# Interleaving two tensors: output rows stored in four pieces of 8 KiB, two tiles taking turns within a row

## The chip, the core and the metric

The kernel runs on one core of a Trainium2 chip. The core has engines that compute (of these only VectorE, called DVE in the profile, does work here), an on-chip memory of 128 partitions (SBUF), and 16 DMA engines that move data between SBUF and the off-chip memory (HBM, "dram" in the names). A transfer is issued by an engine's instruction queue: here SyncE (SP) issues the loads and ScalarE (ACT) the stores. Each issue is spread over the 16 DMA engines, 8 partitions each, and runs beside whatever else they hold. When it has landed, it raises a semaphore by 16, and other engines wait for that.

The metric is the device time of one execution, in microseconds (us).

## The reference

```python
def reference(x, y):                       # each (32, 256, 1024) float32
    batch, seq, dim = x.shape
    result = np.zeros((batch, seq, dim * 2), dtype=np.float32)
    result[..., 0::2] = x
    result[..., 1::2] = y
    return result
```

Element i of x goes to place 2i of the output and element i of y to place 2i + 1. Nothing is calculated: 33.6 MB of x and 33.6 MB of y are read, and 67.1 MB are written, 134.2 MB in all. Since the last dimension is only doubled, the tensors can be taken as flat: flat element j of x and of y becomes the flat output pair (2j, 2j + 1).

## The kernel before

The flat tensors are cut into n = 8 steps (k = 0 to 7). In a step each of the 128 partitions takes W = 8192 consecutive elements of x (a row of 32 KiB), the same of y, and yields 16384 consecutive elements of the output (64 KiB in HBM). SBUF holds two x tiles, two y tiles (b = k % 2) and two output tiles `ot[0]` and `ot[1]`, each 128 x 8192 float32. A step's output doesn't fit one output tile, so it is made in two halves, h = 0 and h = 1: half h takes columns h * 4096 to (h + 1) * 4096 of x and y, fills `ot[h]`, and is stored to the h-th 32 KiB of each 64 KiB output row.

Everything is written out by hand, one queue per kind of work, with semaphores between them:

- SP issues the loads. The first x tile comes as two halves of its columns (L42 and L43, semaphores `xsem[0]` and `hsem`); all other loads are a whole tile of 4 MiB (x at L50, y at L53). From k = 2 on, the x load waits until the third of the four copies of step k - 2 is done, and the y load until the fourth is, because these free the buffers (`woven` counts copies).
- VectorE makes four copies in each step: for each half, x into the even places of `ot[h]` (L67) and y into the odd places (L70). Ahead of the first it waits for the x tile (for h = 0; in the first step, half 1 waits for `hsem`), and, from the second step on, until the store that used `ot[h]` before has landed (`osem[h]`). The y copy of half 0 also waits for the y tile.
- ACT waits for the two copies of a half and issues its store (L83). The very first store is issued as two column ranges, 8 KiB and 24 KiB of each row (L77 and L81), with a semaphore of its own (`qsem`) for the first.

At the end ACT and SP wait for the last stores, and the semaphores are set back. After the program is built, `tile_interleave_kernel` moves the first two SP loads to the front of the program, ahead of the opening barrier.

Of the kernel before, what the change touches and what calls it, by code (L numbers as in the profile page):

```python
# [3 lines left out]


def _interleave(nc, x, y, out):
    P = 128
    W = 8192
    H = W // 2  # L10

    total = 1
    for s in x.shape:
        total *= s
    n = total // (P * W)
    assert n * P * W == total

    def rows(ap, names, k):
        flat = ap.rearrange("b s d -> (b s d)")
        return flat[k * names : (k + 1) * names].rearrange("(p w) -> p w", p=P)  # L20

    fp32 = mybir.dt.float32
    xt = [nc.alloc_sbuf_tensor(f"xt{b}", [P, W], fp32).ap() for b in (0, 1)]
    yt = [nc.alloc_sbuf_tensor(f"yt{b}", [P, W], fp32).ap() for b in (0, 1)]
    ot = [nc.alloc_sbuf_tensor(f"ot{b}", [P, W], fp32).ap() for b in (0, 1)]

    xsem = [nc.alloc_semaphore(f"xsem{b}") for b in (0, 1)]
    hsem = nc.alloc_semaphore("hsem")
    qsem = nc.alloc_semaphore("qsem")
    ysem = [nc.alloc_semaphore(f"ysem{b}") for b in (0, 1)]  # L30
    woven = nc.alloc_semaphore("woven")
    osem = [nc.alloc_semaphore(f"osem{b}") for b in (0, 1)]


    cuts = [0, W // 4, W]
    parts = [slice(a, b) for a, b in zip(cuts, cuts[1:])]

    xs = [rows(x, P * W, k) for k in range(n)]
    ys = [rows(y, P * W, k) for k in range(n)]
    os_ = [rows(out, 2 * P * W, k) for k in range(n)]  # L40

    nc.sync.dma_start(out=xt[0][:, :H], in_=xs[0][:, :H]).then_inc(xsem[0], 16)  # L42
    nc.sync.dma_start(out=xt[0][:, H:], in_=xs[0][:, H:]).then_inc(hsem, 16)  # L43

    for k in range(n):
        b = k % 2
        if k >= 2:
            nc.sync.wait_ge(woven, 4 * (k - 2) + 3)
        if k:
            nc.sync.dma_start(out=xt[b], in_=xs[k]).then_inc(xsem[b], 16)  # L50
        if k >= 2:
            nc.sync.wait_ge(woven, 4 * (k - 2) + 4)
        nc.sync.dma_start(out=yt[b], in_=ys[k]).then_inc(ysem[b], 16)  # L53

    for k in range(n):
        b = k % 2
        for h in (0, 1):
            c = slice(h * H, (h + 1) * H)
            if h == 0:
                nc.vector.wait_ge(xsem[b], 16 * (k // 2 + 1))  # L60
            elif k == 0:
                nc.vector.wait_ge(hsem, 16)
            if k:
                nc.vector.wait_ge(osem[h], 16 * k)
            if (k, h) == (1, 0):
                nc.vector.wait_ge(qsem, 16)
            nc.vector.tensor_copy(out=ot[h][:, 0::2], in_=xt[b][:, c]).then_inc(woven, 1)  # L67
            if h == 0:
                nc.vector.wait_ge(ysem[b], 16 * (k // 2 + 1))
            nc.vector.tensor_copy(out=ot[h][:, 1::2], in_=yt[b][:, c]).then_inc(woven, 1)  # L70

    for k in range(n):
        for h in (0, 1):
            nc.scalar.wait_ge(woven, 4 * k + 2 * h + 2)
            if (k, h) == (0, 0):
                for c in parts[:-1]:
                    nc.scalar.dma_start(  # L77
                        out=os_[k][:, c], in_=ot[h][:, c]
                    ).then_inc(qsem, 16)
                c = parts[-1]  # L80
                nc.scalar.dma_start(out=os_[k][:, c], in_=ot[h][:, c]).then_inc(osem[h], 16)  # L81
                continue
            nc.scalar.dma_start(  # L83
                out=os_[k][:, h * W : (h + 1) * W], in_=ot[h]
            ).then_inc(osem[h], 16)

    nc.scalar.wait_ge(osem[0], 16 * n)
    used = sorted(s.num for s in [*xsem, hsem, qsem, *ysem, woven, osem[0]])
    assert used == list(range(used[0], used[-1] + 1)), used
    nc.scalar.sem_clear(range(used[0], used[-1] + 1))  # L90
    nc.sync.nop(nofuse=True).wait_op(osem[1], 16 * n, "sem-ge").then_inc(
        osem[1], -16 * n
    )


def kernel(tc, x, y, out):
    nc = tc.nc
    tc.close()
    tc.compile()

    _interleave(nc, x, y, out)

    blocks = nc.main_func.blocks
    for engine in (mybir.EngineType.SP, mybir.EngineType.SP):
        opening = blocks[0].instructions
        at, moved = next(
            (b, i)
            for b in blocks[1:]
            for i in b.instructions
            if i.engine == engine and i.opcode == "DMACopy"  # L110
        )
        assert not (moved.sync_info and moved.sync_info.on_wait)
        body = at.instructions
        body.remove(moved)
        gate = next(
            n
            for n, i in enumerate(opening)
            if i.engine == engine and i.opcode == "Drain"
        )
        opening.insert(gate, moved)  # L120
        at.instructions = body
        blocks[0].instructions = opening


# [1 line left out]
_INS = ['x', 'y']  # L126
_OUTS = [((32, 256, 2048), 'float32')]


# [23 lines left out]
```

## Time and profile before

| | us |
|---|---|
| median of 3 runs (lowest, highest) | 314.22 (314.19, 314.39) |
| span of the profiled execution (first to last instruction) | 312.9 |
| VectorE busy, 32 copies | 72.0 |
| one x copy / one y copy, mean | 2.295 / 2.288 |
| VectorE idle, waiting for stores to land | 206.5 |
| store of 4 MiB, issue to landing, median | 34.1 |
| x load / y load of 4 MiB, issue to landing, median | 24.3 / 41.5 |

The profiled execution's own time is known as its span only; the three runs were timed without a profile, and their median is 1.3 us longer than that span. A view of the profile is a page (shares of engines, DMA traffic in 40 slices, the chain of work that ended last, groups of instructions, DMA issues) or an answer of the trace behind it: groups by line, the timeline, tables by stretches of time. "DMA share" is the mean busy share of the 16 DMA engines. The trace also keeps a record of each DMA packet: its queue, start, duration and size. The profile names the loads' queue q1 and the stores' queue q10. "Issue to landing" counts the time in which a transfer waits behind earlier ones.

### The profile page before, as it was taken

To read this page: it belongs to the slowest core of one execution; us is meant where nothing else is said; L and a number is where in the kernel's file an instruction comes from. 1 tells how busy PE (TensorE), PEld (TensorE's weight loads), DVE (VectorE), ACT (ScalarE), POOL (GpSimd) and SP (SyncE) were. 2 spreads that over 40 slices of the span, in tenths; PEclk is the share of its full clock that TensorE was granted. 3 is DMA by queue.
4 is the path that set the end of the run, shared out by engine and by line. 5 is a ranking of instruction groups with operands and counts; after the bars stand their busy time and mean duration, and the time that the engine had idled before them with its cause. 6 is when DMAs were issued, how large, how long until landed. Compare 5 with 4: busy or idle time off the path is not lost.

```text
span 312.9 us, 114 instructions
## 1 busy us (share of the span) xinstructions
DVE 72.0 (23%) x32; POOL 0.2 (0%) x4
## 2 busy tenths in 40 slices
DVE  0216000501305023050220503205032050415410
POOL 0000000000000000000000000000000000000000
DMA  8999999999999999999999999999999999999998
GB/s 337 467 402 436 436 402 419 452 457 415 427 444 411 461 402 469 402 469 402 469 402 465 406 440 432 423 448 402 469 402 469 402 469 402 469 402 448 423 423 381
DMA packets 4896, 134.22 MB, mean 429 GB/s; under 512 B 544, under 2 KB 544, under 8 KB 544
## 3 DMA queue, kind: packets, MB, share of 16 engines
q1 hardware_dynamic: 2448, 67.11, 50.1%
q10 hardware_dynamic: 2448, 67.11, 49.7%
HBM read 67.11 MB, written 67.11 MB: 429 GB/s over the span
## 4 chain that ended last, share of the span: by engine, by line
DMA 82%; DVE 12%; issue 0%
DMA out_dram<-ot 76%; DMA yt<-in_y_dram 6%; DVE ot L70 6%; DVE ot L67 6%
## 5 line engine op out<-in xcount | busy, mean ns | idle before, releaser
L67 DVE COPY ot<-xt 128x4096 f32<-128x4096 f32 x16 | 36.7, 2295 | 213.8 <-DMA out_dram<-ot 206.5
L70 DVE COPY ot<-yt 128x4096 f32<-128x4096 f32 x16 | 36.6, 2288 | 12.3 <-DMA yt<-in_y_dram 12.3
L137 POOL MEMSET const-bfloat16-1.0<- 128x1 bf16 x1 | 0.1, 103 | 0.0
L137 POOL MEMSET const-uint8-127<- 128x1 uint8 x1 | 0.1, 102 | 0.0
L137 POOL MEMSET const-float32-0.0<- 128x1 f32 x1 | 0.1, 100 | 0.2 <-issue 0.2
L137 POOL MEMSET const-float32-1.0<- 128x1 f32 x1 | 0.1, 99 | 0.0
## 6 DMA issues: line engine op xcount, KB each, us to landing
out_dram<-ot ACTq DMA_DIRECT2D x15, 4096.0 KB, 34.1
yt<-in_y_dram SPq DMA_DIRECT2D x8, 4096.0 KB, 41.5
xt<-in_x_dram SPq DMA_DIRECT2D x7, 4096.0 KB, 24.3
xt<-in_x_dram SPq DMA_DIRECT2D x2, 2048.0 KB, 9.5
out_dram<-ot ACTq DMA_DIRECT2D x1, 3072.0 KB, 32.8
out_dram<-ot ACTq DMA_DIRECT2D x1, 1024.0 KB, 16.3
```

What stands on the lines that cost most here:

```text
L67: nc.vector.tensor_copy(out=ot[h][:, 0::2], in_=xt[b][:, c]).then_inc(woven, 1)
L70: nc.vector.tensor_copy(out=ot[h][:, 1::2], in_=yt[b][:, c]).then_inc(woven, 1)
L137: nc = _bacc.Bacc("TRN2", target_bir_lowering=False, num_devices=1)
```

## The change

The two output tiles of a step no longer hold the first and the second half of each output row. The 64 KiB of a row are seen as S = 4 groups of two pieces of 8 KiB (G = 2048 elements): `ot[0]` holds the first piece of every group and `ot[1]` the second. Accordingly half h copies, from x and from y, four runs of 1024 elements that lie 2048 elements apart. So a store still reads one contiguous row of 32 KiB per partition in SBUF, but writes four pieces of 8 KiB that lie 16 KiB apart in HBM.

The store is issued through a new function, `_split_copy`, which builds the DMA instruction itself, with the SBUF side described as one row of 8192 elements and the HBM side as four pieces of 2048. The first store is still issued in two parts: the first piece of each row by the ordinary call, and then three pieces (one read of 24 KiB, three writes) by `_split_copy`. Since half 0 of the first step now takes elements from the whole x tile, the first copy waits for both halves of the first x load. The number and order of the instructions on every queue stay as they were.

```diff
+def _split_copy(engine, out, in_):
+
+    return engine.add_instruction(
+        mybir.InstDMACopy(
+            mode="Copy",
+            name=engine.bass.get_next_instruction_name(),
+            engine=engine.engine,
+            ins=engine.lower_ap_dma(in_.rearrange("p (o w) -> p o w", o=1)),
+            outs=engine.lower_ap_dma(out),
+            queue=QUEUES[engine.engine],
+        )
+    )
...
+    S = 4
+    G = W // S
...
-    os_ = [rows(out, 2 * P * W, k) for k in range(n)]
+    os_ = [
+        rows(out, 2 * P * W, k).rearrange("p (s h g) -> p s h g", h=2, g=G)
+        for k in range(n)
+    ]
...
-            c = slice(h * H, (h + 1) * H)
+            pairs = ot[h].rearrange("p (s w two) -> p s w two", s=S, two=2)
+            xc, yc = (
+                t[b].rearrange("p (s h w) -> p s h w", s=S, h=2)[:, :, h] for t in (xt, yt)
+            )
             if h == 0:
                 nc.vector.wait_ge(xsem[b], 16 * (k // 2 + 1))
-            elif k == 0:
-                nc.vector.wait_ge(hsem, 16)
+                if k == 0:
+                    nc.vector.wait_ge(hsem, 16)
...
-            nc.vector.tensor_copy(out=ot[h][:, 0::2], in_=xt[b][:, c]).then_inc(woven, 1)
+            nc.vector.tensor_copy(out=pairs[:, :, :, 0], in_=xc).then_inc(woven, 1)
...
-            nc.vector.tensor_copy(out=ot[h][:, 1::2], in_=yt[b][:, c]).then_inc(woven, 1)
+            nc.vector.tensor_copy(out=pairs[:, :, :, 1], in_=yc).then_inc(woven, 1)
...
             if (k, h) == (0, 0):
-                for c in parts[:-1]:
-                    nc.scalar.dma_start(
-                        out=os_[k][:, c], in_=ot[h][:, c]
-                    ).then_inc(qsem, 16)
-                c = parts[-1]
-                nc.scalar.dma_start(out=os_[k][:, c], in_=ot[h][:, c]).then_inc(osem[h], 16)
-                continue
-            nc.scalar.dma_start(
-                out=os_[k][:, h * W : (h + 1) * W], in_=ot[h]
+                nc.scalar.dma_start(out=os_[k][:, 0, h], in_=ot[h][:, :G]).then_inc(
+                    qsem, 16
+                )
+                first = 1
+            _split_copy(
+                nc.scalar, os_[k][:, first:, h], ot[h][:, first * G :]
             ).then_inc(osem[h], 16)
```

## The prediction

> **What bounds the kernel now.** I read the page's head and its DMA part first.
>
> ```profile
> span 312.9 us, 114 instructions
> ...
> DVE 72.0 (23%) x32; POOL 0.2 (0%) x4
> ...
> DMA  8999999999999999999999999999999999999998
> GB/s 337 467 402 436 436 402 419 452 457 415 427 444 411 461 402 469 402 469 402 469 402 465 406 440 432 423 448 402 469 402 469 402 469 402 469 402 448 423 423 381
> DMA packets 4896, 134.22 MB, mean 429 GB/s; under 512 B 544, under 2 KB 544, under 8 KB 544
> ...
> q1 hardware_dynamic: 2448, 67.11, 50.1%
> q10 hardware_dynamic: 2448, 67.11, 49.7%
> ```
>
> VectorE works 23% of the span and the 16 DMA engines all of it: the loads' queue (q1) and the stores' queue (q10) take half each, 99.8% together. Second, the table of stretches, which splits that by phase (columns: length, VectorE, GpSimd, TensorE clock, DMA share, GB/s):
>
> ```profile
> 0.00:2.00 2.00, 0.00 (x0) 0.20 (x4) 1.00 0.59 131
> ...
> 100.00:138.72 38.72, 8.99 (x5) 0.00 (x0) 1.00 1.00 433
> 138.72:177.44 38.72, 8.98 (x5) 0.00 (x0) 1.00 1.00 433
> 177.44:216.16 38.72, 8.99 (x5) 0.00 (x0) 1.00 1.00 433
> ```
>
> One step of the loop (16.78 MB) takes 38.72 us with every DMA engine full. Third, the timeline at the end, and the issues with their time to landing:
>
> ```profile
> 283.90 2.30 DVE L67 COPY ot<-xt 128x4096 f32<-128x4096 f32 x1 [8.95 <-DMA out_dram<-ot]
> 286.11 2.29 DVE L70 COPY ot<-yt 128x4096 f32<-128x4096 f32 x1
> 293.53 2.29 DVE L67 COPY ot<-xt 128x4096 f32<-128x4096 f32 x1 [5.14 <-DMA out_dram<-ot]
> ```
>
> ```profile
> out_dram<-ot ACTq DMA_DIRECT2D x15, 4096.0 KB, 34.1
> yt<-in_y_dram SPq DMA_DIRECT2D x8, 4096.0 KB, 41.5
> ```
>
> VectorE's long waits for stores mean only that it is early: when an output tile lands, the other one is already queued behind it. The packet records of the trace, which the views only sum up, say the same engine by engine: data moves from 1.07 to 312.55 us without a hole, then 0.35 us pass until the last landing. So the time is the sum of the packets' service on one DMA engine, and the change is worth what it does to that sum, plus any hole it opens.
>
> The records give the prices. A 32 KiB packet starts 1209.4 ns after the one before it (recorded duration 1213 ns; neighbours overlap by some 4 ns), a 16 KiB packet 607.1 ns (611). Two 16 KiB packets are thus 4.8 ns dearer than one of 32 KiB: a packet costs 4.8 ns beside its bytes. An 8 KiB packet (the first store has eight per engine) is recorded at 309 ns; its starts are 303 to 311 ns apart, and the rule gives 306.0. Check: a step is 4 tiles x 8 rows = 32 packets x 1209.4 ns = 38.70 us, against 38.72. The whole, per engine: loads 16 x 607.1 + 120 x 1209.4 ns = 154.84 us; stores 120 x 1209.4 + 8 x 306.0 + 8 x 908.3 ns (the 24 KiB ones, by the same rule) = 154.84 us; 34 completion packets at about 6 ns, 0.2 us; the slow first packets of the loads, 0.62 us, and slow load packets when the first store joins (59 on 16 engines, mostly at 26 to 31 us), 0.56 us. With 1.07 and 0.35 us at the ends that is 312.5 us, against a span of 312.9. The three times have a median of 314.22, so 1.3 us lie outside the span, and I keep them.
>
> **The change part by part.**
>
> 1. *Stores write four pieces per row.* Per DMA engine the stores before are 120 + 8 + 8 = 136 data pieces; after, 16 tiles x 8 rows x 4 = 512, so 376 more. If a written piece is charged as the trace charges a packet, that is 376 x 4.8 ns = +1.80 us. The trace has no transfer whose read and write sides are cut differently, so the price has bounds: nothing, if the four pieces ride in the packet of the one 32 KiB read; and (4 x 309 - 1213) / 3 = 7.7 ns each, if the recorded durations don't overlap, 2.9 us in all. Below nothing I find no row: no smaller packet here is cheaper per byte than a larger one. All DMA engines are full in every stretch, so no cover hides a nanosecond of this. I take 1.80 us, because the nearest row (two 16 KiB packets against one of 32 KiB in one queue) has the writes cut as well as the reads, and no row shows a cut for free.
>
>    The Trainium skill, page "DMA: Bandwidth & Descriptors", section "Why small descriptors are slow (HBM only)", puts a fixed cost of about 3 cycles on each packet between the read and the write side, and says that joining consecutive descriptors into one packet amortizes it. At that page's 850 MHz, an estimate, 376 packets would cost 1.3 us; joined ones, nothing. The trace's 4.8 ns is of the same kind and a little larger.
>
> 2. *The first copy waits for both halves of the first x tile.* Its start moves from 7.33 us to the second half's landing at 12.25 (issued at 0.42, 11.8 us to landing). Behind it stands the y copy, which waits for y until 21.89 in any case: cover 12.28 us of idle VectorE. Cost nothing; without the cover 4.9 us of a later first store, which the loads queued on SP (16 MB are on order from 2.75 us on) would still fill.
>
> 3. *Copies read four runs of 1024 and write a strided row.* Same element count, 32 copies of 2.29 us. The trace shows no copy with a two-level source. Bounds: 2.29 us, or about 4.4 us (twice the 2.2 us from one start to the next) if such a source halved VectorE's rate. Nearest row is the present copy, whose destination is strided already: I take 2.29. The cover is thinnest at the end: a tile lands at 283.88, its successor is issued at 288.4 and is needed when the other tile's data ends, 293.2; with 1.07 us from issue to first packet (the first load's) 3.7 us are spare. At half rate the two copies take 4.4 us more: a hole of 0.7 us, once.
>
>    The Trainium skill, page "VectorE: DVE Perf Modes", section "What auto-detection actually checks", grants the two-port mode where the outermost non-unit dimensions of source and destination are even; four runs satisfy that. The trace agrees as far as it goes: 4096 elements in 2.29 us, 1.8 per ns.
>
> 4. *ACT's issues.* Still 17, in the same order, one per tile plus the first piece. Their 0.34 us may grow with more write pieces; the same 3.7 us cover it, and in the shared phase, where a tile is issued some 15 us before its data can start, far more. Cost nothing. SP's queue is not touched: its x loads wait for the third copy of the step two before, its y loads for the fourth, as now.
>
> 5. *Turns between the queues.* Today a 32 KiB load and a 32 KiB store alternate on each engine. If a store piece counted as a packet of its own, loads would take 1209 of every 1515 ns (1209 + 306), end sooner in each step (16 packets x 1.515 = 24.2 us), and stores would run alone for the other 14.5 us. The sum of bytes is unchanged. The handovers between tiles then happen with no load beside them, as at the end of the trace now, with the same 3.7 us spare. Cost nothing; with the latency that the first store shows beside loads (issue 24.24, first packet 28.71: 4.5 us) the spare shrinks to 0.3 us but stays.
>
> Sum: 314.22 + 1.80 = 316.0 us, +0.57%. A change below 0.2% (0.63 us) is about what these measurements can't tell from none; the three runs spread over 0.20 us.
>
> **The rivals.**
>
> *Pieces ride in the row's packet (not slower).* The place is the write side of each store. The read of a row stays one piece, and if the packet is the read, its 4.8 ns is paid once per row as now. It decides below 0.63 us / 376 = 1.7 ns per piece. For it: the edit goes out of its way to keep one read, and loads and stores today alternate read by read. Against: no row shows a written cut without a read cut. Time: 314.22, or 0.04 less, since the first tile's rows read in two pieces on both sides. It is also what the page's sentence on joined descriptors would give.
>
> *A new wait.* Turns as in part 5, together with copies at half rate: a hole of 0.7 us at the handover in every step rather than once, 7 x 0.7 = 4.9 us on top of 1.80, so about 321 us. Half rate alone gives 316.7. Or the slow load packets come back: if the 0.56 us at the first store's eight 8 KiB packets were due to their size, at 70 ns each, 512 would cost 36 us; but between 31 and 39 us the same mixture ran at 1213 ns per load, so it is rather the joining of the queue. The full VectorE row (16 copies between 2286 and 2298 ns) speaks against the first.
>
> *Faster.* Only the 0.56 and the 0.62 us of slow first packets are there to be won; without both, 313.0. Nothing in the edit touches the loads that show them, though the first store's pieces lie beside one group.
>
> *The change doesn't do what it says.* If reads are cut to 8 KiB too, each row is four packets by either count, and the time is that of the forecast, 316.0, with the turns of part 5.
>
> **How the numbers follow.** Pieces charged one by one, reads cut or not: 0.52, 316.0, its own range 315.4 (3.2 ns) to 317.1 (7.7 ns). Pieces in the row's packet: 0.30, within 0.2%. A new wait, or a larger price per piece: 0.11, from 316.7 up. Faster: 0.07. So slower 0.52 + 0.11 = 0.63, same 0.30, faster 0.07. The range goes from 313.9 (the second case with 0.3 us of scatter) to 318.0 (7.7 ns per piece and the 0.7 us hole, 317.8); outside lie the faster case and most of the long waits, some 0.15.
>
> **What would show it.** Right: a step period of 38.72 + 48 x 0.0048 = 38.95 us at 431 GB/s with the DMA share still at 1.00; store packets of 8 KiB, 2048 of them per four tiles. The rival: 38.72 us again, store packets of 32 KiB. A new wait: a DMA share under 1.00 in some stretch, or copies over 2.4 us. The landings tell the turns: if x loads land in clearly less than 24.3 us from issue, the store pieces count as packets in the alternation. Wrong altogether if the period moves while packets and copies keep their durations.

## The result, and the profile after

The changed kernel takes 314.80 us (median of 16 runs, 314.72 to 314.95) against 314.20 us (16 runs, 314.12 to 314.39) before: a ratio of 1.002, with a 95% interval of 1.0012 to 1.0027. It is 0.6 us slower, a third of the 1.8 us that was forecast, and just under the 0.63 us that the prediction took as the bound between "no change" and "slower".

The page's head and DMA part of the changed kernel:

```profile
span 313.4 us, 115 instructions
...
DVE 72.0 (23%) x32; POOL 0.2 (0%) x4
...
DMA  8999999999999999999999999999999999999997
...
DMA packets 4896, 134.22 MB, mean 428 GB/s; under 512 B 544, under 2 KB 544, under 8 KB 544
...
q1 hardware_dynamic: 2448, 67.11, 50.0%
q10 hardware_dynamic: 2448, 67.11, 49.8%
...
L92 DVE COPY ot<-xt 128x4096 f32<-128x4096 f32 x16 | 36.7, 2295 | 219.2 <-DMA out_dram<-ot 206.8
...
xt<-in_x_dram SPq DMA_DIRECT2D x7, 4096.0 KB, 24.4
```

The number of packets is the same as before, 4896. So a store packet is a read of 32 KiB, however its writing is cut, and the x loads still land 24.4 us after their issue: loads and stores take turns row by row as before. VectorE's copies kept their 2295 ns.

The timeline of the kernel before, at two successive steps:

```profile
96.31 2.30 DVE L67 COPY ot<-xt 128x4096 f32<-128x4096 f32 x1 [14.98 <-DMA out_dram<-ot]
...
135.03 2.30 DVE L67 COPY ot<-xt 128x4096 f32<-128x4096 f32 x1 [14.98 <-DMA out_dram<-ot]
```

The timeline of the changed kernel, at the x copies of three successive steps and at the last one:

```profile
57.55 2.29 DVE L92 COPY ot<-xt 128x4096 f32<-128x4096 f32 x1 [28.82 <-DMA out_dram<-ot]
...
96.32 2.29 DVE L92 COPY ot<-xt 128x4096 f32<-128x4096 f32 x1 [14.96 <-DMA out_dram<-ot]
...
135.12 2.29 DVE L92 COPY ot<-xt 128x4096 f32<-128x4096 f32 x1 [14.96 <-DMA out_dram<-ot]
...
293.98 2.30 DVE L92 COPY ot<-xt 128x4096 f32<-128x4096 f32 x1 [5.16 <-DMA out_dram<-ot]
```

Up to 96.32 us nothing is lost. From there a step takes 38.80 us in place of 38.72, and the last copy starts at 293.98 in place of 293.53: 0.45 us lost by then, and 0.1 in the last two stores. The packet records place the loss: load packets kept 1213 ns (median), while store packets went to 1218 ns, and to 1219 ns once no loads are left. But the first 12 whole store rows of each engine still have 1213 ns.

### The profile page after: what moved, and what is told of

Same layout as the page of the kernel before. It is cut to its first block, busy times and chain, and to the rows that moved or that the text cites. A ratio compares the mean times of both kernels' runs of the same rounds, so it can differ in the third digit from the quotient of the medians.

```text
span 313.4 us, 115 instructions
## 1 busy us (share of the span) xinstructions
DVE 72.0 (23%) x32; POOL 0.2 (0%) x4
## 2 busy tenths in 40 slices
DMA packets 4896, 134.22 MB, mean 428 GB/s; under 512 B 544, under 2 KB 544, under 8 KB 544
## 3 DMA queue, kind: packets, MB, share of 16 engines
q1 hardware_dynamic: 2448, 67.11, 50.0%
q10 hardware_dynamic: 2448, 67.11, 49.8%
## 4 chain that ended last, share of the span: by engine, by line
DMA 82%; DVE 12%; issue 0%
DMA out_dram<-ot 76%; DMA yt<-in_y_dram 6%; DVE ot L95 6%; DVE ot L92 6%
## 5 line engine op out<-in xcount | busy, mean ns | idle before, releaser
L92 DVE COPY ot<-xt 128x4096 f32<-128x4096 f32 x16 | 36.7, 2295 | 219.2 <-DMA out_dram<-ot 206.8
## 6 DMA issues: line engine op xcount, KB each, us to landing
xt<-in_x_dram SPq DMA_DIRECT2D x7, 4096.0 KB, 24.4
```

Source lines behind the costliest of these rows:

```text
L92: nc.vector.tensor_copy(out=pairs[:, :, :, 0], in_=xc).then_inc(woven, 1)
```

## Experiments

Each kernel ran beside the kernel before on the same chip. "A row alone" is the time from one 32 KiB store row to the next at the end of the span, where no loads are left, from the packet records (the starts of the last two tiles, divided by 8 rows; completion packet included). "Step" is the time from one step to the next between the starts of the same tile's packets, or between landings; the two agree but for the run with two pieces.

| stores (or loads) as | time, us | ratio to before (95%) | step, us | row alone, ns |
|---|---|---|---|---|
| before: 1 piece | 314.2 | | 38.725 | 1210.2 |
| 2 alternating pieces | 314.34 | 1.0005 (0.9995 to 1.0014) | 38.725 | 1210.2 |
| 4 alternating (the change) | 314.80 | 1.002 (1.0012 to 1.0027) | 38.795 | 1215.9 |
| 4 adjacent | 314.79 | 1.0018 (1.0009 to 1.0028) | 38.795 | 1215.9 |
| 8 adjacent | 315.97 | 1.0057 (1.004 to 1.0074) | 38.946 | 1225.3 |
| 8 alternating | 322.49 | 1.0264 (1.0249 to 1.0279) | uneven | 1330.1 |
| 16 alternating | 318.42 | 1.0133 (1.0118 to 1.0148) | 39.247 | 1244.1 |
| 64 adjacent | 331.78 | 1.0561 (1.0543 to 1.0578) | 41.054 | 1357.1 |
| stores: reads cut in 4 too | 317.98 | 1.0126 (1.0111 to 1.0141) | uneven | 1224.3 |
| loads and stores: reads cut in 4 | 317.93 | 1.0122 (1.0107 to 1.0137) | 39.176 | 1224.3 |
| loads write 4 spaced pieces | 315.79 | 1.0051 (1.0036 to 1.0066) | 38.91 | |
| loads write 4 adjacent pieces | 316.76 | 1.008 (1.0065 to 1.0095) | 39.00 | |

### Two, eight and sixteen pieces

The edit to the changed kernel, with S = 2, 8 and 16; the first store's first part takes F pieces so that it stays at 8 KiB (16 KiB for S = 2):

```diff
-    S = 4
+    S = 2        # 8, 16
+    F = max(1, S // 4)
...
-                nc.scalar.dma_start(out=os_[k][:, 0, h], in_=ot[h][:, :G]).then_inc(
+                _split_copy(nc.scalar, os_[k][:, :F, h], ot[h][:, : F * G]).then_inc(
                     qsem, 16
                 )
-                first = 1
+                first = F
```

> Two pieces of 16 KiB per row in place of four of 8 KiB (the first store's two parts are 16 KiB each). Three theories on the extra 0.6 us. LARGER SIDE: an engine reads and writes in parallel; the read side needs 1204.7 + 4.8 ns per 32 KiB read, the write side about 2.7 ns per written piece beside the same 1204.7 ns, and the slower side sets the pace; then (2 + 1) x 2.7 = 8.1 ns per pair of a store row and a load row stays under the reads' 9.6 ns: no more than before, within 0.05 us, store packets recorded at 1213 ns. PER PIECE: each piece beyond the first adds 1.5 ns: 120 x 1.5 = +0.18 us over before, store packets at 1214 to 1215 ns. PER CUT ROW: a row that is cut at all costs about 4.7 ns: +0.55 us as with four pieces, packets at 1218 ns.

Measured: 314.34 us, an interval that includes no change; store packets at 1213 ns, a step of 38.725 us by the packet starts and a row alone of 1210.2 ns, both exactly as before. (The copies start 38.74 to 38.75 us apart, because the last engine's landing comes some 20 ns later from step to step, 0.1 us in all.) This run has all else of the change (the wait for both halves of x, copies from runs spaced apart, the store built by hand). So none of that costs anything, and a cut by itself is not what costs: the theory of a price per cut row falls.

> Eight pieces of 4 KiB per row. LARGER SIDE: pair of rows 2409.4 + 9 x 2.7 = 2433.7 ns against 2418.9, for some 98 pairs, and 1204.7 + 8 x 2.7 - 1209.5 = 16.8 ns on some 29 store rows that run alone: 1.45 + 0.49, +1.9 us over before, some 316.1 us, store packets at about 1230 ns. PER PIECE: 888 x 1.5 ns = +1.3 us, 315.5 us. PER CUT ROW: +0.55 us, 314.8 us.

Measured: 322.49 us, far outside all three. Three steps in the middle of the span take 38.97 to 38.99 us from copy to copy, near the 38.96 of the first theory (16 x 2433.7 ns, and 0.02 us of completion packets). The two steps before them take 40.99 and 39.46 us: there some store packets take up to 1900 ns. Store rows that run alone take 1330 ns on average, but unevenly: of an engine's eight rows of a tile three or four take some 1480 ns, the others 1228. A later run takes this up.

> Sixteen pieces of 2 KiB per row. LARGER SIDE: pair 2409.4 + 17 x 2.7 - 2418.9 = 36.4 ns for 98 pairs, 1204.7 + 16 x 2.7 - 1209.5 = 38.4 ns for 29 rows: 3.57 + 1.11, +4.7 us over before, some 318.9 us, store packets at about 1250 ns. PER PIECE: 1912 x 1.5 ns = +2.9 us, 317.1 us. PER CUT ROW: +0.55 us.

Measured: 318.42 us, nearest to the larger side (318.9), 1.3 us above a price per piece and 3.6 above a price per cut row. The rows alone now give the price: (1244.1 - 1215.9) / 12 = 2.35 ns per piece. With it, the write side takes 1205.9 ns plus 2.35 ns per piece for a row (1215.9 ns, less 0.6 for the completion packet and 4 x 2.35), and the read side 1209.5 ns. For 2 pieces that is 1210.6, as good as equal to the reads. That is why four pieces cost 0.6 us and two cost nothing.

The chain in order of time, of the run with sixteen pieces: two x copies one step apart, 39.25 us.

```profile
116.63 2.29 DVE ot L93
...
155.88 2.29 DVE ot L93
```

### Four, eight and sixty-four adjacent pieces

These go back to the kernel before, its tiles, copies and places in HBM, and change its 15 whole-tile stores alone:

```diff
-            nc.scalar.dma_start(
-                out=os_[k][:, h * W : (h + 1) * W], in_=ot[h]
+            _copy(                       # builds the DMA like _split_copy, sides as given
+                nc.scalar,
+                os_[k][:, h * W : (h + 1) * W].rearrange("p (s g) -> p s g", s=4),   # 8, 64
+                ot[h].rearrange("p (o w) -> p o w", o=1),
             ).then_inc(osem[h], 16)
```

> The kernel before, with its tiles, copies and places in HBM; only its 15 whole-tile stores write each 32 KiB row as four pieces of 8 KiB that lie next to each other (one read of 32 KiB). The runs so far fit a write side of 1205.9 ns per row plus 2.35 ns per written piece, against a read side of 1204.7 + 4.8 ns per read. LARGER SIDE: the cut alone brings the cost: +0.55 us over before, step period 38.80 us, store packets at 1218 ns. PLACE: the cost is of the alternating places in HBM: no more than before, 38.72 us and 1213 ns. The same as before would also come out if adjacent pieces were joined to one on the way.

Measured: 314.79 us, a step of 38.795 us, store packets at 1218 ns: the changed kernel in every number, without its places in HBM. The cost is the cut, not the turns that the tiles take. Two x copies, one step apart (38.79 us):

```profile
115.56 2.30 DVE ot L86
...
154.35 2.29 DVE ot L86
```

> As the run with four adjacent pieces, but eight of 4 KiB. The run with eight pieces in alternating places came to 322.5 us, far over the 316.1 expected; its step period in the middle of the span fits 2.35 ns per piece, while store rows that run alone took 1335 ns. PLACE OF 4 KiB PIECES: one tile touches only every other 4 KiB of HBM there, and here it touches all: then only the piece price is left, step period 38.95 us, 98 x 13.8 ns + 29 x 15.2 ns = +1.8 us, some 316.0 us. SIZE: if 4 KiB pieces are slow by themselves, about 322 us again.

Measured: 315.97 us and a step of 38.946 us, as expected of the piece price. So eight pieces of 4 KiB cost 1.8 us when they are adjacent, and the other 6.5 us of the alternating run come with its places in HBM. The two runs near the end in the table of stretches (columns: length, VectorE, GpSimd, TensorE clock, DMA share, GB/s), alternating first:

```profile
290.00:300.00 10.00, 3.98 (x2) 0.00 (x0) 1.00 0.99 390
300.00:310.00 10.00, 4.50 (x2) 0.00 (x0) 1.00 1.00 396
```

```profile
290.00:300.00 10.00, 4.50 (x2) 0.00 (x0) 1.00 0.98 419
300.00:310.00 10.00, 0.00 (x0) 0.00 (x0) 1.00 0.98 419
```

The DMA share is practically the same; the alternating run moves less in it, because its packets take longer.

> The kernel before with each 32 KiB row of its whole-tile stores written as 64 adjacent pieces of 512 bytes, far outside the sizes that the piece price was fitted on. LARGER SIDE with 2.35 ns per piece: a pair of rows 2411.8 + 65 x 2.35 = 2564.6 ns, step period 16 x 2564.6 + 20 = 41.05 us; 98 pairs x 145 ns + 29 store rows x 147 ns = +18.5 us over before, some 332.7 us. If small pieces carry a further cost, it is longer.

Measured: a step of 41.054 us against 41.05 expected, and rows alone of 1357.1 ns: (1357.1 - 1244.1) / 48 = 2.35 ns per piece again, down to pieces of 512 bytes. The time, 331.78 us, is 0.9 us under the sum, which counted the first tile's rows as cut; its 8 rows per engine are not, and 8 x 145 ns is 1.2 us. Three x copies, one step apart:

```profile
119.08 2.29 DVE ot L86
...
160.13 2.29 DVE ot L86
...
201.18 2.30 DVE ot L86
```

### Reads cut too

First the stores' reads alone, in the changed kernel:

```diff
-            _split_copy(
-                nc.scalar, os_[k][:, first:, h], ot[h][:, first * G :]
+            nc.scalar.dma_start(
+                out=os_[k][:, first:, h],
+                in_=ot[h].rearrange("p (s g) -> p s g", g=G)[:, first:],
             ).then_inc(osem[h], 16)
```

> The changed kernel with its stores issued by the ordinary call, so that reads and writes are both cut into pieces of 8 KiB. The prediction put this at the same price as cut writes: 376 more packets x 4.8 ns = +1.8 us over before, 316.0 us. The LARGER SIDE theory says the same (the read side then needs 4 x 306 = 1224 ns per row, more than the write side), so that the prediction's price was one of read packets. Store packets appear as 8 KiB ones, and loads take four of five turns' time: the x loads land in about 13 us from issue in place of 24. If the handovers between tiles are late then, with the stores running alone for 14 us of each step, the DMA share falls below 1.00 and the time goes above 316.5 us.

Measured: 317.98 us, 2.0 us over the sum. The packets are now of 8 KiB:

```profile
DMA packets 10912, 134.22 MB, mean 424 GB/s; under 512 B 544, under 2 KB 544, under 8 KB 544
...
q10 hardware_dynamic: 8464, 67.11, 50.3%
```

The x loads land after 16.8 us in place of 24.3 (13 was expected). So the loads of a step end early, and the stores run alone until the next loads start. The packet records place the surplus there. No load packet starts between 68.0 and 87.9 us, and where loads join the stores again packets are slow: load packets of up to 2448 ns in place of 1213, and store packets of up to 789 ns in place of 309, 1.25 us per engine in all. The later pauses cost some 0.3 us together. The table of stretches shows the place: the engines are as busy as ever there, but move less.

```profile
56.00:86.00 30.00, 9.00 (x4) 0.00 (x0) 1.00 0.99 423
86.00:93.00 7.00, 0.00 (x0) 0.00 (x0) 1.00 1.05 373
93.00:100.00 7.00, 0.00 (x0) 0.00 (x0) 1.00 0.99 428
```

The 16 engines drift apart too: one store's landings on them spread over up to 3.2 us, where before they spread over 0.25. No handover was late for it: between the first microseconds and the last, the gaps between packets add up to 0.02 us per engine. Only at the end does it show, where the last landings lie 0.8 us apart in place of 0.25.

Then the loads as well, so that turns are equal again. The x and y tiles get 64 bytes between pieces, so that the pieces stay apart:

```diff
-    xt = [nc.alloc_sbuf_tensor(f"xt{b}", [P, W], fp32).ap() for b in (0, 1)]
+    xt = [
+        nc.alloc_sbuf_tensor(f"xt{b}", [P, 4 * (W // 4 + 16)], fp32)
+        .ap()
+        .rearrange("p (s g) -> p s g", s=4)[:, :, : W // 4]
+        for b in (0, 1)
+    ]                                    # yt alike
...
-            nc.sync.dma_start(out=xt[b], in_=xs[k]).then_inc(xsem[b], 16)
+            nc.sync.dma_start(out=xt[b], in_=cut(xs[k])).then_inc(xsem[b], 16)
```

> The run with cut reads and writes of the stores, and now the loads are cut into 8 KiB packets too (tiles with 64 bytes between the pieces), so that loads and stores take turns of the same size again. That run came to 318.0 us, 1.9 us above 376 x 4.8 ns. TURNS: the surplus came from loads and stores taking turns of unequal size; here it goes, and 752 more packets than before cost 752 x 4.8 ns = 3.6 us: some 317.9 us, with x loads landing in about 24 us. PRICE PER PACKET: if a cut packet costs 10 ns, 752 x 10 = 7.5 us: some 321.7 us.

Measured: 317.93 us, as the turns theory says, though there are twice as many additional packets as in the run before it. So 4.8 ns is the price of a packet, that is, of a read: a row alone takes 1224.3 ns in both runs, 4 x 306, where cut writes alone gave 1215.9. The surplus of the run before went with the unequal turns; here the loads never pause before their end, and no packet after 45 us is slow. Whether unequal turns cost anything without such pauses was not tried. The x loads land after 42.9 us rather than 24, and the stores after 30.8 rather than 34.1: with small packets in both queues the stores run ahead and the loads lag further behind. That was not foreseen, and did not show in the time.

### Loads that write pieces

The last pair asks whether 2.35 ns is the price of any written piece. In the kernel before, each load (L50, L53) reads a row in one piece and writes four (the half loads, L42 and L43, two), first with 64 bytes between them in SBUF (tiles as just shown), then adjacent:

```diff
-            nc.sync.dma_start(out=xt[b], in_=xs[k]).then_inc(xsem[b], 16)
+            _copy(nc.sync, xt[b], one(xs[k])).then_inc(xsem[b], 16)         # spaced
+            _copy(nc.sync, four(xt[b]), one(xs[k])).then_inc(xsem[b], 16)   # adjacent
```

> The kernel before, but it is the loads that read a row of 32 KiB in one piece and write four pieces of 8 KiB, into x and y tiles with 64 bytes between the pieces in SBUF; stores as before. WRITE SIDE IN GENERAL: the pair of rows needs 2 x 1205.9 + 5 x 2.35 = 2423.6 ns of writing as in the changed kernel: step period 38.80 us, load packets at about 1218 ns, +0.5 us over before. WRITES TO HBM ALONE: no change, 38.72 us, load packets at 1213 ns.

> The kernel before, but the loads write each row as four pieces of 8 KiB that lie next to each other in SBUF (one read of 32 KiB; the two half loads two pieces each). The run with 64 bytes between the pieces came to 315.8 us and a step of 38.91 us, against 314.7 and 38.80 expected; its load packets ran from 1213 to 1236 ns, so that the offset of 64 bytes may have had a price of its own. WRITE SIDE IN GENERAL: step period 38.80 us, load packets at 1218 ns without scatter, +0.5 us over before. WRITES TO HBM ALONE: 38.72 us. If it comes to 38.91 us again, pieces written to SBUF are dearer than pieces written to HBM.

Measured: 315.79 and 316.76 us, steps of 38.91 and 39.00 us, where 38.80 was expected. Cut writes of a load are not free, and cost more than those of a store. By the step of 39.00 us a pair of rows takes (39.00 - 0.02) us / 16 = 2436 ns, and (2436 - 2 x 1205.9 - 2.35) / 4 is 5.5 ns per piece. But load rows that run alone, before the first store, take 1242 ns from start to start when the pieces are adjacent and 1233 ns when they are spaced, and (1242 - 1205.9) / 4 is 9.0. Two more rows of the packet records speak against any fixed price of a written piece here. The half loads, which write two pieces of 8 KiB per read of 16 KiB, kept the 607 ns that they take in the kernel before. And in the run with all reads cut, which writes the same spaced pieces, a load row alone takes 4 x 306 = 1224 ns: less than the 1233 ns with the read left whole. So the larger of two sides, which fits the stores, does not account for these loads. The spaced pieces were the cheaper ones, so the 64 bytes do not explain it. Why loads with whole reads and cut writes cost this much stays open.

No run suggests a version faster than the kernel before: a single piece per row is the least that both sides can have at this row size. Stores that read several pieces and write one were not tried.

## Why the prediction was wrong

*The time as a sum of packets.* Right. The DMA share stayed at 1.00 to 1.01, no hole opened, and what was lost is what store packets gained: store packets average 1217.4 ns in the records against 1213.0, so 120 x 4.4 ns = 0.53 us per engine, of 0.56 us that the span grew.

*Part 1, the price of a piece: the step that failed.* Its term of +1.80 us measured 0.6. The prediction took 4.8 ns for each of 376 pieces because the trace's nearest row, two 16 KiB packets against one of 32 KiB, "has the writes cut as well as the reads". That row could not tell the two sides apart, and its price is that of a read. The run with all reads cut confirms the 4.8 ns for cut reads (317.93 against 317.9). A piece that a store writes costs 2.35 ns, on another side of the engine that works at the same time and had slack. The landings show this side: in the last two tiles, where no loads are left, a landing comes 370 ns (median) after the end of the engine's last packet before, and 426 to 434 ns after it with four, eight, sixteen or sixty-four pieces. The writes fall some 60 ns behind, however many the pieces, and then hold the reads to their own pace. Per pair of a load row and a store row the reads need 2 x 1209.5 = 2419 ns. The writes need 2 x 1205.9 + 5 x 2.35 = 2423.6 ns. Only the difference, 4.6 ns a pair, shows while loads run, and 1215.3 - 1209.5 = 5.8 ns a row when stores run alone.

With some 98 pairs and 29 rows alone that makes 0.45 + 0.17 = 0.62 us; the first rows, which cost nothing until the writes lag by some 70 ns (last section), take 0.07 off it, and the span grew by 0.56. The two constants of the write side, 1205.9 and 2.35 ns, are a fit to the runs with four and sixteen pieces; the steps with eight (38.946 us) and sixty-four (41.054 us) were then forecast from them and came out so. The sum should have been the larger of two sides instead of one side plus all extras.

*The Trainium skill on small descriptors.* The Trainium skill, page "DMA: Bandwidth & Descriptors", section "Why small descriptors are slow (HBM only)", has joined descriptors share the fixed cost of one packet. The trace agrees as far as the packet goes: 4896 packets, cut or not. Read as the prediction read it, that would leave the pieces free, and here they are not: from 4 to 64 pieces per row each costs 2.35 ns, since the write side is then the slower one.

*The rival "pieces ride in the row's packet".* Its mechanism is what the profile shows: 4896 packets, turns as before, x loads at 24.4 us. Its time, 314.2, lacked the write side; its bound of 1.7 ns per piece was just kept, 0.56 us / 376 = 1.5 ns on average, which owes something to the number of pieces: with eight adjacent ones the same mechanism costs 1.8 us. It had 0.30 and the forecast 0.52, and the profile before has no transfer whose writes alone are cut, which would have told them apart.

*The rival "reads are cut too" and part 5.* Both were given the forecast's 316.0, with the turns at "cost nothing". The run with cut reads came to 317.98, 2.0 us more. The handovers held, as part 5 says: no engine stood idle. What part 5 put at nothing is that loads which end early must join the stores anew, and of the surplus 1.25 us arose at the first such place. The prediction had the slow packets of a joining queue among its rivals, but not in this one.

*Parts 2, 3 and 4.* Right at no cost: the first copy moved to 12.39 us (12.25 forecast) and the y copy behind it still waited for y; copies stayed at 2.29 us; the run with two pieces has all of this, and its interval includes no change.

*New waits, a gain.* Neither came. The slow packets of the beginning are there as before (0.52 us per engine for the loads that run when stores join, against 0.56).

## What to carry to other kernels

For stores like these, price an engine that reads and writes at once by its slower side, and ask of every row in a trace which of the two sides it priced. A cut of the writes is free until it makes their side the slower one: here two pieces per 32 KiB row were free, four were not. In a kernel whose DMA engines are full, cutting only the writes of a store is cheaper than cutting its reads as well (314.8 against 318.0 us): a cut read costs 4.8 ns, and the reads also set the turns between the queues. Don't carry this to loads: a load row alone took 1233 ns with the writes cut and 1224 with both cut.

## What had not been expected of the hardware

- The price of a written piece to HBM is 2.35 ns from 4 to 64 pieces per row, with no bend (rows alone: 1215.9, 1225.3, 1244.1 and 1357.1 ns for 4, 8, 16 and 64).
- The write side may lag the read side for a while before the records show it. The first slow store row comes after 15 cut rows of four adjacent pieces (15 x 4.6 = 69 ns) and after 5 rows of eight (5 x 14 = 70 ns, with 2 x 1205.9 + 9 x 2.35 - 2419 = 14 ns a pair); the first row of 64 is recorded at 1279 ns, 72 less than the 1351 of the next. The same lag in all three suggests a fixed store of some 1.9 KB, an estimate from these counts at 27.2 bytes per ns (32,768 bytes in 1204.7 ns).
- Pieces of 4 KiB, 8 KiB apart, cost 6.5 us more than adjacent ones of that size; pieces of 2 KiB, 4 KiB apart, and of 8 KiB, 16 KiB apart, cost nothing for their place (1244.1 ns on the line of the adjacent ones; 1215.9 ns for both). Why only that spacing is slow was not settled.
- A load row that is read whole and written to SBUF in four pieces takes 1242 ns alone (adjacent) or 1233 ns (64 bytes apart), against 1209 ns written whole, and 1224 ns when its reads are cut too. Why the whole read makes it dearer is open.
